# Two weights' low parts by accumulating DMA, and the decay table's sums one and a half products earlier, in a one-core Mamba-2 and band-attention step

## The chip, the cores and the metric

The program runs on 1 core of one Trainium2 chip. The metric is the time of one execution in microseconds (us), taken on the device; several executions are timed and their median is given. One more execution is profiled: its trace holds every instruction with start and duration, and all trace numbers below are from that one. Engines: PE is TensorE (matmuls; PEld its weight loads), DVE is VectorE, ACT is ScalarE, POOL is GpSimd, SP is the queue from which most DMAs are issued. Each engine works its own instructions in the order in which they were given to it.

## What is computed

A two-layer hybrid encoder advances one step: 1024 frames of a new stream and 64 frames of a running one, 1088 columns together, all in f32. Layer 0 is a Mamba-2 SSD mixer and a SwiGLU FFN, layer 1 is chunk-band attention and a SwiGLU FFN, with a shared K/V in between. The change lies at the head of layer 0:

```python
zxbcdt = u @ w_in                       # u = rmsnorm(x): z, x, B, C and dt are slices of it
conv = conv_b
for k in range(CONV_W):
    conv = conv + padded[:, k:k + L] * conv_w[k]
xbc = jax.nn.silu(conv)
...
dt = jax.nn.softplus(dt_raw + dt_bias)
dA = dt * A
Acs = jnp.cumsum(dA, axis=-1)           # within a chunk
Lm = jnp.exp(jnp.where(causal, Acs[..., :, None] - Acs[..., None, :], -jnp.inf))
y_diag = jnp.einsum('bcgjqs,bcsgjp->bcqgjp', CB[:, :, :, None] * Lm, xd)
decay_to_end = exp(Acs[..., -1:] - Acs)
chunk_states = einsum(Bc, xd * decay_to_end)
y_off = einsum(Cc, h_prev) * exp(Acs)
```

The tables of `dt`, of the sums `Acs` and of the decays are needed before any head's SSD work can begin.

## The kernel before, in words

**Products.** TensorE takes operands in a short format (float32r). So each f32 operand is split in a high part (rounded by ScalarE) and a low part (what is left over), and a product is three matmuls for each of the 8 blocks of the inner dimension: high weight by high u (L454), high weight by low u (L455), low weight by high u (L456), in this order. A *unit* is one 128-row weight tile by one slice of columns, 24 matmuls. There are three slices s = 0, 1, 2 with 384, 384 and 320 columns. A unit's result stands in one PSUM bank; the tag `mm` has two such banks, taken in turn, and the next unit that takes a bank must wait until the evacuation has read it. `scaled` (L721) evacuates: it multiplies the bank by the norm's row and writes SBUF. In slice 2 it takes two instructions for x, B and C, one for the new stream's 256 columns and one for the running stream's 64.

**Weights.** The class `Weights` streams weight tiles: SP loads a tile of 128x1024 f32 (512 KB) into one of two `raw` buffers (L252), ScalarE casts it to the high part (L340), VectorE subtracts to the low part (L341), both into one of three `hl` buffers; the `raw` buffer is free once both have read it. An `hl` buffer is free once the last unit that uses the weight is done. A weight planned with `acc` takes another way, in `part`: ScalarE casts (L334) and then writes minus the high part into the low part's place (L335), and GpSimd issues a DMA (L336) that reads the tile from HBM once more and adds it there. In the kernel before only the first weights of the FFNs are planned so, 12 tiles in all.

**Order of the weights.** First B0, C0 and x0 (in `w_in` the tiles 32, 36 and 16), all of which run slice by slice with the dt product between them. Then the groups of `order`: group 0 is x1 and z0, group 1 is x2 and z1, and so on. For group 0 the units come as x1 s0, x1 s1, z0 s0, z0 s1, z0 s2, x1 s2. x1's buffer is the one that B0 leaves, z0's the one that C0 leaves, x2's the one that x0 leaves.

**Order on TensorE.** TensorE's order is written out by hand: `Stream` keeps a planned time `st.t`, each unit adds its columns' cost to it, and at the half and the end of every unit side tasks whose due time has come put their instructions in between. A task yields its cost and the delay until its next step. The orders of the other engines are laid by a planner over the whole program, from its own costs, with priorities (`tc.high_priority`); it fills idle places with later instructions.

**The decay table.** `table_task` is such a side task. Its first step stands in the middle of B0's unit of slice 2: matmuls that turn the dt rows into columns (L678), and then, on VectorE at high priority, softplus (a polynomial of nine steps, L688, and L689 to L691, which write `t0`, the product of dt and A). It yields 1.0 with the delay `TB_V`. Its second step takes the sums, a matmul with a triangle of ones (`acsp`, L694), and VectorE copies them (`nac`, L696); 1.0 later the third takes the totals (`lastp`, L699) and nine transposes (`acT`, L707), whose rows ScalarE copies (L709) and SP stores to HBM (`ascr`, L710). 2.5 after that `tabs` lets the SSD tasks go.

**The SSD tasks.** `ssd_task(j, s)`, for head pair j and slice s, counted by q = 3j + s, first loads the sums' rows spread over the partitions (`MT`, L845, and `ea`, L848), makes decays of them (VectorE L854, ScalarE L855), and 8.0 later transposes x (`xtp`, L866), scales it (`xd`, VectorE L876; `xe`, GpSimd L877), masks the decays (`MT` by `CB`, L878), multiplies to the chunk states (`sp`, L885), and for two tasks at a time gives out the results (`yp` L816, `yo` L826). x1 s2's unit may not stand in TensorE's order before the results of q = 0 and q = 1. B and C are transposed and multiplied by `group_task` (`bnp` L785, `cbp` L791).

Of the kernel before, what the change touches and what calls it, by code (L numbers as in the profile page):

```python
# [44 lines left out]
AT_W1, AT_W2 = 6.0, 2.5  # L45
SSD_GAP, SSD_D = 4.4, 8.0
ST_W, ST_RB = (6.5, 22.0, 22.0), (6.0, 1.0, 1.0)
TB_W, TB_V = 1.0, 14.0
ES = 0.5, 0.5, 0.0
OS = 1.9, 1.4  # L50
EP_W, ER_W, EQ_W = (9.4, 9.4, 2.2), (8.9, 8.9, 3.3), (11.0, 11.0)
# [323 lines left out]
def hybrid_kernel(  # L375
# [28 lines left out]
    for _ in range(17):  # L404
# [14 lines left out]
    W = Weights(  # L419
        nc, Ring(wp, "raw", RAWB, [P, 1024]), Ring(wp, "hl", HLB, [P, 2, 1024], F32R),  # L420
        Ring(None, "half", 0, [P, 2, 512], F32R), Ring(None, "tt", 0, [P, 1024]),
    )
# [134 lines left out]
    order = []  # L557
# [8 lines left out]
            else:  # L566
                order.append((("x", 15), ("z", 14), ("z", 15)))
    W.plan(*[dict(src=[w_in[t]]) for t in (32, 36, 16)])
    for grp in order:
        W.plan(*[dict(src=[w_in[{"B": 32, "C": 36, "x": 16, "z": 0}[kd_] + i]]) for kd_, i in grp])  # L570

    MGS = ((0, 1, 2), (3, 4, 5), (6, 7))
    for b in range(2):
# [64 lines left out]
    with ExitStack() as es:  # L638
# [440 lines left out]
        for grp in order:  # L1079
# [9 lines left out]
            for i, s in seq:  # L1089
                kd_, jj_ = grp[i]  # L1090
# [5 lines left out]
                elif kd_ == "C" and q >= 5:  # L1096
                    g_, s_ = divmod(q - 5, 3)
# [904 lines left out]
```

## Time and profile before

| | |
|---|---|
| median of 3 runs | 2980.72 us (2979.49 to 2980.98) |
| the profiled execution | 2979.66 us, of which the trace's span is 2978.0 us |
| granted TensorE clock, mean over the span | 0.996 |
| busy share of the span | PE 98%, DVE 69%, ACT 47%, POOL 24% |
| instructions in the span | 56302 |

A busy PE is not a PE at its peak: matmuls that run at a lower granted clock count as busy too. Shares over the whole span say little about the stretch around the change, from 50 to 110 us, which is why the next part reads windows. In a list of instructions in order of time a row gives start, duration, engine, line, operation, what is written and read, how many were merged (x6), and in brackets the idle time of the engine before it and what ended that. In a list of waits a row gives who waited for whom, the total in us, the number of times and the longest. In a table of windows a row gives the stretch, its length, then for each engine its busy time and number of instructions, then TensorE's granted clock, the busy share of the DMA engines, and GB/s.

### The profile page before, as it was taken

The numbers are of one execution on the slowest core, as the hardware profiler recorded it, in microseconds if no ns is written. First come the engines' busy times: TensorE is split into PE (matmuls) and PEld (weight loads), VectorE is DVE, ScalarE is ACT, GpSimd is POOL, SyncE is SP. The second block draws the span as 40 slices with busy tenths as digits, with TensorE's granted clock in tenths as the row PEclk, the third lists the DMA queues.
The fourth block names the chain that finished last, engine by engine and source line by source line (L and its number), as shares of the span: only waits on it lengthen the run. The fifth ranks groups of instructions, "written<-read, shape, count | busy, mean of one in ns | idle before, by whom it ended". The sixth has DMA issues, their size and how long they took to land.

```text
span 2978.0 us, 56302 instructions
## 1 busy us (share of the span) xinstructions
PE 2921.0 (98%) x21626; PEld 2871.4 (96%) x21626; DVE 2040.2 (69%) x4471; ACT 1394.1 (47%) x2530; POOL 719.2 (24%) x821
## 2 busy tenths in 40 slices
PE   8999999999999999999999999999999999999999
PEld 7899999999999999999999899999999999999999
DVE  7887878885768545584567777777678645475544
ACT  6554646454453223344445665555653323244443
POOL 1333333331122343451111000000131343351111
PEclk9999999999999999999999999999999999999999
DMA  3333333244563222345665222223365222255654
GB/s 122 113 105 99 102 100 106 90 120 148 171 185 113 82 81 73 96 153 171 202 192 157 83 80 73 65 64 95 115 180 174 80 81 75 78 153 174 215 178 137
DMA packets 201551, 363.36 MB, mean 122 GB/s; under 512 B 20545, under 2 KB 149281, under 8 KB 201281
## 3 DMA queue, kind: packets, MB, share of 16 engines
q1 hardware_dynamic: 199488, 353.39, 38.6%
q0 software_dynamic: 1792, 6.36, 1.1%
q8 instruction: 170, 2.79, 0.4%
q14 instruction: 101, 0.82, 0.1%
HBM read 292.47 MB, written 62.74 MB: 119 GB/s over the span
## 4 chain that ended last, share of the span: by engine, by line
PE 83%; DVE 9%; DMA 3%; ACT 2%; issue 2%; POOL 0%; SPq 0%; DVEq 0%; ACTq 0%; POOLq 0%
PE px L1280 9%; PE px L1281 9%; PE px L1282 9%; PE mm L454 7%; PE mm L456 7%; PE mm L455 7%; PE po L1480 6%; PE po L1481 6%; PE po L1479 6%; PE mmx L455 3%; PE mmx L454 3%; PE mmx L456 3%; PE po L1763 2%; PE ptp L1724 1%; DVE sc L1702 1%
## 5 line engine op out<-in xcount | busy, mean ns | idle before, releaser
L454 PE MATMUL mm<-r,hl 128*128 128x384 f32 (+2 forms) x1664 | 555.2, 334 | 5.7 <-ACT BT L768 3.0
L456 PE MATMUL mm<-r,hl 128*128 128x384 f32 (+2 forms) x1664 | 539.0, 324 | 3.6 <-DVE hl L353 2.9
L455 PE MATMUL mm<-r,hl 128*128 128x384 f32 (+2 forms) x1664 | 537.8, 323 | 0.0
L341 DVE TENSOR_TENSOR hl<-raw,hl 128x1024 fp32r<-128x1024 f32 (+1 forms) x219 | 257.6, 1177 | 227.5 <-ACT hl L340 223.2
L1281 PE MATMUL px<-r,hl 128*128 128x288 f32 (+1 forms) x1184 | 347.3, 293 | 0.0
L454 PEld LDWEIGHTS mm<-r,hl 128*128 128x128 f32 x1664 | 314.7, 189 | 8.8 <-ACT BT L768 3.2
L456 PEld LDWEIGHTS mm<-r,hl 128*128 128x128 f32 x1664 | 313.9, 189 | 5.1 <-DVE hl L353 3.9
L455 PEld LDWEIGHTS mm<-r,hl 128*128 128x128 f32 x1664 | 315.0, 189 | 0.1
L1280 PE MATMUL px<-r,hl 128*128 128x288 f32 x1056 | 310.9, 294 | 0.0
L1282 PE MATMUL px<-r,hl 128*128 128x288 f32 x1056 | 310.7, 294 | 0.0
L340 ACT CAST hl<-raw 128x1024 fp32r<-128x1024 f32 (+1 forms) x219 | 219.9, 1005 | 176.1 <-PE po L1481 99.7
L480 POOL TENSOR_TENSOR ssum<-ssum,sq 128x256 f32<-128x256 f32 (+3 forms) x97 | 129.2, 1333 | 639.6 <-ACT sq L479 624.3
L1281 PEld LDWEIGHTS px<-r,hl 128*128 128x128 f32 x1184 | 222.3, 188 | 0.0
L1282 PE MATMUL px<-rx,hl 128*128 128x256 f32 x768 | 214.9, 280 | 6.6 <-DVE hl L341 6.6
L1280 PE MATMUL px<-rx,hl 128*128 128x256 f32 x768 | 215.4, 280 | 0.8 <-ACT hl L340 0.8
L1480 PE MATMUL po<-rx,hl 128*128 128x384 f32 (+1 forms) x624 | 201.5, 323 | 0.2 <-DVE rx L1344 0.2
L1280 PEld LDWEIGHTS px<-r,hl 128*128 128x128 f32 x1056 | 198.4, 188 | 0.2 <-DVE u L1295 0.2
L1282 PEld LDWEIGHTS px<-r,hl 128*128 128x128 f32 x1056 | 198.3, 188 | 0.0
L1479 PE MATMUL po<-rx,hl 128*128 128x384 f32 (+1 forms) x608 | 197.3, 324 | 0.0
L1481 PE MATMUL po<-rx,hl 128*128 128x384 f32 (+1 forms) x608 | 196.5, 323 | 0.0
L1281 PE MATMUL px<-rx,hl 128*128 128x256 f32 x640 | 178.7, 279 | 0.0
L290 POOL TENSOR_TENSOR tt<-raw 128x512 f32<-128x512 f32 x40 | 55.4, 1386 | 438.3 <-DMA raw<-in_w_f_dram 333.9
(359 smaller groups left out, 8052.6 us busy)
## 6 DMA issues: line engine op xcount, KB each, us to landing
raw<-in_w_f_dram SPq DMA_DIRECT2D x154, 512.0 KB, 3.8
rx<-in_w_f_dram SPq DMA_DIRECT2D x54, 512.0 KB, 3.7
raw<-in_w_in_dram SPq DMA_DIRECT2D x40, 512.0 KB, 3.6
MT<-ascr SPq DMA_DIRECT2D x48, 384.0 KB, 4.3
sg<-hscr SPq DMA_DIRECT2D x88, 192.0 KB, 3.5
raw<-in_w_f_dram SPq DMA_DIRECT2D x44, 384.0 KB, 3.4
raw<-in_w_so_dram SPq DMA_DIRECT2D x32, 512.0 KB, 4.0
raw<-in_w_kv_dram SPq DMA_DIRECT2D x18, 512.0 KB, 3.5
```

What stands on the lines that cost most here:

```text
L340: self.nc.scalar.copy(h, v)
L341: (eng or self.eng or self.nc.vector).tensor_tensor(lo, v, h, op=ALU.subtract)
L454: PE.matmul(ps[:, :n], h_, xh, start=(first and i == 0), stop=False)
L455: PE.matmul(ps[:, :n], h_, xl, start=False, stop=False)
L456: PE.matmul(ps[:, :n], l_, xh, start=False, stop=(last and i == nk - 1))
L480: (eng or G).tensor_tensor(ssum[:, :n], ssum[:, :n], q[:, :n], op=ALU.add)
L1280: PE.matmul(ps, wh, ah[:, k, :], start=(k == 0), stop=False)
L1281: PE.matmul(ps, wh, al[:, k, :], start=False, stop=False)
L1282: PE.matmul(ps, wl, ah[:, k, :], start=False, stop=(k == 3))
L1479: PE.matmul(ps[:, :n], wh, xh, start=(k == 0), stop=False)
L1480: PE.matmul(ps[:, :n], wh, xl, start=False, stop=False)
L1481: PE.matmul(ps[:, :n], wl, xh, start=False, stop=(k == FT - 1))
```

## The change

Two edits. The x1 and z0 weights (group 0 of `order`) are planned with `acc`: their low parts come by the way of L335 and L336 in place of L341. And the delay `TB_V` between the table's first and second step goes from 14.0 to 10.0 of the planned time, which changes the place of the sums, and of all that follows from them, in TensorE's order.

```diff
-TB_W, TB_V = 1.0, 14.0
+TB_W, TB_V = 1.0, 10.0
...
     W.plan(*[dict(src=[w_in[t]]) for t in (32, 36, 16)])
-    for grp in order:
-        W.plan(*[dict(src=[w_in[{"B": 32, "C": 36, "x": 16, "z": 0}[kd_] + i]]) for kd_, i in grp])
+    for g_, grp in enumerate(order):
+        W.plan(*[dict(src=[w_in[{"B": 32, "C": 36, "x": 16, "z": 0}[kd_] + i]], acc=g_ < 1) for kd_, i in grp])
```

The way that `acc` takes in `part` is in the kernel before already:

```python
        if it.get("acc"):
            with self.tc.high_priority(self.pri):
                self.nc.scalar.copy(h, v)
                self.nc.scalar.activation(lo, h, AF.Copy, scale=-1.0)
            self.nc.gpsimd.dma_start(lo, it["src"][0], accum_op=ALU.add)
            it[key] = h, lo
            return
```

## The prediction

> **What bounds the kernel now.** I read the page's chain first, then TensorE's waits in the stretch that the change touches (30 to 115 us), then windows of 3.41 us around these waits for the granted clock, then each engine's instructions in order of time.
>
> ```profile
> PE 83%; DVE 9%; DMA 3%; ACT 2%; issue 2%; POOL 0%; SPq 0%; DVEq 0%; ACTq 0%; POOLq 0%
> ```
>
> The chain that ends last is TensorE's for 83%. VectorE's work costs time only where TensorE waits for it, and time that TensorE saves early shortens the whole. Its waits between 30 and 115 us:
>
> ```profile
> PE sp L885 <- POOL xe L877: 3.7, 1, 3.7
> PE mm L454 <- ACT BT L768: 3.0, 1, 3.0
> ...
> PE sp L885 <- DVE xd L876: 1.8, 1, 1.8
> ```
>
> Two places, then: 3.0 us at the start of x1 s0, and 3.7 + 1.8 = 5.5 us at the first chunk states. Each is followed by a stretch at a lower clock (busy time, PEclk, DMA share, GB/s):
>
> ```profile
> 65.69:69.10 3.41, 0.57 (x4) 1.00 0.45 154
> 69.10:72.51 3.41, 3.26 (x13) 0.65 0.54 159
> 72.51:75.92 3.41, 3.41 (x21) 0.85 0.00 0
> 99.79:103.20 3.41, 1.59 (x12) 0.66 0.00 0
> 103.20:106.61 3.41, 3.41 (x29) 0.50 0.01 2
> 106.61:110.02 3.41, 3.41 (x27) 0.84 0.93 210
> ```
>
> Busy time by the missing clock is what the low clock cost: 3.26 x 0.35 + 3.41 x 0.15 = 1.65 us behind the first wait, 1.59 x 0.34 + 3.41 x 0.50 + 3.41 x 0.16 = 2.8 us behind the second. So 13.0 us are at stake in all: 4.65 at the first place, 8.3 at the second.
>
> **The first wait.** The engines in order of time:
>
> ```profile
> 66.21 0.41 DVE L721 TENSOR_TENSOR craw<-mm,rb 128x256 f32<-128x256 f32 x1
> ...
> 67.38 1.23 DVE L341 TENSOR_TENSOR hl<-raw,hl 128x1024 fp32r<-128x1024 f32 x1 [0.39 <-ACT hl L340]
> ...
> 68.89 0.22 DVE L721 TENSOR_TENSOR craw<-mm,rb 128x64 f32<-128x64 f32 x1
> ...
> 69.25 0.41 PE L454 MATMUL mm<-r,hl 128*128 128x384 f32 x1 [2.99 <-ACT BT L768]
> ...
> 69.67 0.34 PE L456 MATMUL mm<-r,hl 128*128 128x384 f32 x1
> ```
>
> The list names ScalarE's BT, but x1 s0 neither reads nor writes BT. It takes the bank that C0 had, and that bank's last reader is the 64-column evacuation, 68.89 + 0.22 = 69.11. The evacuation is late because VectorE does x2's low part (67.38) before it, and that had to wait for x0's end; its other half was late (66.21) because of x1's and z0's low parts and the table's polynomial.
>
> **The second wait:**
>
> ```profile
> 78.16 0.65 PE L694 MATMUL acsp<-tt,U 128*128 128x288 f32 x2
> 82.75 1.27 SPq L710 DMA_DIRECT2D ascr<-row  x3
> 84.79 0.38 SPq L845 DMA_DIRECT2D MT<-ascr  x1
> 94.48 1.27 DVE L854 TENSOR_SCALAR MT<-MT,nac 128x128 f32<-128x128 f32 x6 [0.27 <-DMA MT<-ascr]
> 95.06 0.82 PE L866 MATMUL xtp<-ident,xsT 128*128 128x128 f32 x6
> 97.97 1.01 DVE L876 TENSOR_TENSOR xd<-xtp,dt 128x384 f32<-128x384 f32 x2
> 98.67 2.34 POOL L877 TENSOR_TENSOR xe<-xd,dec 128x384 f32<-128x384 f32 x2 [16.59 <-DVE xd L876]
> 99.56 0.94 PE L885 MATMUL sp<-xe,Bn 128*128 128x128 f32 x6 [3.68 <-POOL xe L877]
> 102.63 1.62 PE L885 MATMUL sp<-xe,Bn 128*128 128x128 f32 x6 [1.82 <-DVE xd L876]
> ```
>
> xd waits on VectorE behind the decays (L854), which wait for MT's loads, which follow from the sums at 78.16.
>
> **Edit 1, the low parts.** Removed: two L341 on VectorE. Added: two negations on ScalarE, two DMA issues on GpSimd, two more reads of 512 KB.
>
> ```profile
> 58.62 1.05 ACT L340 CAST hl<-raw 128x1024 fp32r<-128x1024 f32 x1 [1.41 <-PE mmp L456]
> 59.57 0.65 ACT L759 ACTIVATE BT<-craw,pcs 128x323 f32<-128x323 f32 x1
> 60.29 1.22 DVE L341 TENSOR_TENSOR hl<-raw,hl 128x1024 fp32r<-128x1024 f32 x1
> 63.86 1.23 DVE L341 TENSOR_TENSOR hl<-raw,hl 128x1024 fp32r<-128x1024 f32 x1 [0.31 <-ACT hl L340]
> 66.69 0.35 POOL L755 COPY cst<-craw 128x3 f32<-128x3 f32 x1 [7.12 <-DVE craw L721]
> 70.56 0.45 DVE L691 TENSOR_TENSOR tt<-dt,negA 128x288 f32<-128x288 f32 x1
> ACT hl L340 <- PE mm L456: 5.0, 2, 2.6
> ```
>
> VectorE gains 1.22 + 1.23 + 0.31 of waiting = 2.8 us ahead of C0's evacuation. Brought forward by 2.8, the 64 columns would end at 66.3, when TensorE gets there; and x2's low part, which waits for x0's end, then stands behind them. So this wait goes, at the latest part of it. If the planner still puts x2 first, nothing is gained here: bounds 0 and 3.0. The two negations (1.04 each) fall into ScalarE's 5.0 us of waiting between the casts, GpSimd is idle for 7.12 us: both cost nothing there, and if that cover were gone ScalarE would be 2.1 later with slice 2's BT and CT, which TensorE takes up only at x1 s1. The `raw` buffer is free after the cast already, so x2's and z1's loads start 1 to 2 us earlier; nobody waits for these.
>
> What is late next is x1's own low part, which the third matmul of x1 s0 (69.67 now) needs. From the FFN's tiles:
>
> ```profile
> L335 ACT ACTIVATE hl<-hl x7: 1042/1043/1060, 853.8 to 2239.1; 128x1024 fp32r<-128x1024 f32 x7
> L336 POOL DMA_DIRECT2D hl<-in_w_f_dram x7: 849/867/876, 855.1 to 2240.5; - x7
> DMA to landing us min/median/max: 5.8/8.9/11.1
> raw<-in_w_in_dram SPq DMA_DIRECT2D x10, 512.0 KB, 3.9
> 61.50:67.30 5.80, 4.76 (x33) 4.50 (x31) 5.18 (x12) 2.05 (x2) 0.35 (x1) 1.00 0.46 135
> 2209.23:2215.03 5.80, 5.73 (x44) 5.76 (x45) 5.20 (x22) 4.73 (x9) 2.77 (x5) 1.00 0.92 228
> ```
>
> Cast to 59.67, BT (L759) slipped in between to 60.2, negation to 61.2, issue at 61.5. The landing is bounded by 3.9 (a plain load of the same tile) and 11.1. I take 5.8, the FFN's fastest, since it is the nearest: the other DMAs beside it took a share of 0.92, here they take 0.46. So the low part is there at 67.3 (65.4 to 72.6), and the third matmul starts 69.67 - 67.3 = 2.4 us earlier (3.0 earlier, when no wait is left, to 2.9 later). I book 2.3, and the 1.65 of clock, since 0.6 us of idle is left in place of 3.0. z0's low part (cast 4 us later) is needed two units later: nothing.
>
> The Trainium skill, "DMA: Bandwidth & Descriptors", section "Anatomy of one DMA", gives a DMA from GpSimd as 2.0 us plus the bytes over 436 GB/s, for 512 KB an estimate of 3.2 us. By that nothing is left of the wait and the sum below is 0.7 larger; the trace's own 5.8 to 11.1 for such a transfer disagree, and I go by them.
>
> **Edit 2, the sums.** In planned time, counted from the table's first step: its cost 1.0, B0's second half 1.63, C0 3.25, x0 3.25, x1 s0's first half 1.95 make 11.09. Due at 1.0 + 10 = 11.0, the sums now stand in the middle of x1 s0, ahead of `bnp`. Due at 15.0 they missed that place and x1 s0's end (14.02 with bnp and cbp), and came in the middle of x1 s1 (15.97). The totals and transposes go from x1 s1's end to x1 s0's end, `tabs` to the middle of x1 s1, with it the four MT and eight ea loads on SP, and the first `xtp` from z0 s2's end to the middle of z0 s1. The second xtp and the sp stay. No instruction is added.
>
> ```profile
> 72.47 0.84 PE L785 MATMUL bnp<-ident,BT 128*128 128x128 f32 x3
> ```
>
> So acsp moves from 78.16 to 72.47, 5.7 us ahead. Its input t0 was ready at 70.56 + 0.45 = 71.0, and 2.8 us earlier without the low parts, while the middle of x1 s0 comes at about 69: no wait. SP's queue holds nothing that would stop the stores and loads there, GpSimd's neither. The last decays, 94.48 + 1.27 now (one more task's follows), are done some 5 us sooner, ahead of xtp's 95.06. The first sp then finds its xe ready (its xtp stands 1.5 units ahead). The second needs xtp, xd (0.5), xe (2.34 / 2 = 1.2), about 1.9 with the handing over, beside 0.94 + 0.41 us of the first sp and the third xtp on TensorE: 0.6 left; I take 1.0, for VectorE is crowded there. 5.5 - 1.0 = 4.5 us. With 1.0 us idle I expect the clock to hold: 2.8 more. Bounds: 0 (VectorE holds xd as before) and 8.3.
>
> The Trainium skill, "TensorE: Matmul & The Clock Gate", section "Why this matters for your kernels", allows idle gaps of up to about 3 us before the clock falls. By that rule the first stretch's 1.65 us wouldn't be the 2.99 us gap's and would stay: a sum smaller by 1.65. The rows speak against it, 1.00 before that gap and 0.65 behind it.
>
> **The sum.** 2.3 + 1.65 + 4.5 + 2.8 = 11.25. From this comes what VectorE gives back once TensorE runs ahead: it is nearly full behind this stretch, and TensorE's waits there are of this size.
>
> ```profile
> 110.00:150.00 40.00, 40.00 (x296) 39.25 (x295) 37.79 (x98) 23.38 (x34) 18.91 (x27) 1.00 0.43 131
> PE xtp L866 <- DVE nv L498: 2.4, 3, 0.8
> ```
>
> I take 1.5 (0 to 2.4). 9.7 us remain. The profiled execution took 2979.66, 1.66 of it outside the span; 2969.9 follows, and as the median of the runs is 1.06 above the profiled one, 2971.0.
>
> **The rivals.**
> *x1's low part comes late.* At 11.1 us, or with the issue put behind the copy at 66.69 in GpSimd's order, the third matmul starts at 72.6: 2.9 lost, no clock back, the second place's 7.3 less 1.5 stays: 2.9 gained, 2978. Against it: the FFN's slow ones ran beside a full DMA. 17%.
> *VectorE holds the first states.* 5 us earlier sums do nothing if xd still stands behind decays in VectorE's order and a wait of 3.5 us with its low clock stays. Then the second place gives 5.5 - 3.5 = 2 of its 8.3, the first 3.95, less 1.5: 4.5 gained, 2976. For it: 37.79 of 40 us. 15%.
> *Slower: the planner lays the SSD loop anew.* VectorE's, ScalarE's and GpSimd's orders come from one plan, which starts from other times now. If in the loop of 48 SSD tasks TensorE meets one more short wait at each, such as the xtp waits on the norm's steps (three in 290 us now, up to 0.8), 0.2 us a task eat the 9.7; at 0.5 us the loss is 24 - 9.7 = 14 and the time 2995. Against it: TensorE's order in the loop keeps its places, since all due times shift together. 10%.
>
> **How the numbers follow.** The forecast has 58%, its own range 2967.8 (13.0 gained, nothing given back) to 2974. The range, 2966 to 2979.5, takes in the first two rivals and 2 us of a luckier plan. 0.2% is 6 us, about what a measurement can tell. Faster by that: nearly all of the forecast, a fifth of the two small-gain rivals, 61%; within it 33%; slower 6%.
>
> **What would show it.** Right: the 64-column evacuation ahead of x2's low part on VectorE; TensorE's wait at x1 s0 under 1.5 us, on the accumulating DMA; acsp in the middle of x1 s0; MT loads near 77 us; waits before sp of 1 us in all; the clock 1.00 from 66 to 110. Wrong: that DMA landing after 69.7, xd still behind the decays, or new waits in the loop after 110 us.

## The result, and the profile after

The changed kernel takes 2971.76 us, the median of 7 runs (2970.04 to 2976.18); the kernel before, run beside it, takes 2981.54 us, the median of 7 (2979.49 to 2983.44). The ratio is 0.9969, with an interval of 0.9959 to 0.9979: 9.2 us less, between 6 and 12. The profiled execution took 2972.53 us. The prediction was 2971.0 us (2966.0 to 2979.5).

The page of the kernel after, busy time, share and instructions of each engine:

```profile
PE 2920.7 (98%) x21626; PEld 2871.0 (97%) x21626; DVE 2033.7 (68%) x4469; ACT 1395.0 (47%) x2532; POOL 715.7 (24%) x823
```

Nothing in these shares tells of 9 us. TensorE's waits between 30 and 115 us do (a row of 2.4 us at `nbp` and one of 1.0 at `craw`, both ahead of the stretch that the change touches, are left out):

```profile
PE xtp L866 <- ACT zs L948: 1.0, 1, 1.0
...
PE sp L885 <- DVE hn L898: 0.6, 1, 0.6
PE cbp L791 <- DVE Bn L786: 0.4, 1, 0.4
PE mm L456 <- DMA hl<-in_w_in_dram: 0.3, 1, 0.3
```

Of 8.5 us of waiting at the two places, 1.9 are left: 0.34 at x1 s0 and 1.57 before the chunk states. A new wait of 0.35 stands at `cbp`.

**The first place.** The engines of the kernel after, in order of time (this profiled execution came to the table's first matmul, L678, 0.65 us later than the one of before: 54.20 against 53.55, so its times compare with those shown of before after taking off 0.65):

```profile
59.30 1.05 ACT L334 CAST hl<-raw 128x1024 fp32r<-128x1024 f32 x1 [1.44 <-PE mmp L456]
60.25 0.66 ACT L759 ACTIVATE BT<-craw,pcs 128x323 f32<-128x323 f32 x1
60.81 1.04 ACT L335 ACTIVATE hl<-hl 128x1024 fp32r<-128x1024 f32 x1
...
62.16 0.90 POOL L336 DMA_DIRECT2D hl<-in_w_in_dram  x1 [1.92 <-ACT hl L335]
...
64.67 0.22 DVE L721 TENSOR_TENSOR craw<-mm,rb 128x64 f32<-128x64 f32 x1
...
66.76 0.34 PE L454 MATMUL mm<-r,hl 128*128 128x384 f32 x1
67.61 0.44 PE L456 MATMUL mm<-r,hl 128*128 128x384 f32 x1 [0.34 <-DMA hl<-in_w_in_dram]
68.14 0.46 DVE L691 TENSOR_TENSOR tt<-dt,negA 128x288 f32<-128x288 f32 x1
68.52 1.22 DVE L341 TENSOR_TENSOR hl<-raw,hl 128x1024 fp32r<-128x1024 f32 x1
69.46 0.65 PE L694 MATMUL acsp<-tt,U 128*128 128x288 f32 x2
```

C0's last evacuation ends at 64.9, almost 2 us before TensorE begins x1 s0 at 66.76, and x2's low part (68.52) now stands behind it and behind `t0` (L691) as well. What TensorE waits for is x1's own low part, 0.34 us. `acsp` finds `t0` ready: 68.14 + 0.46 = 68.6, needed at 69.46. How long the two accumulating DMAs took from issue to landing (line L336 of the kernel after, between 55 and 75 us; the shorter one is x1's, issued at 62.16):

```profile
DMA to landing us min/median/max: 5.4/6.0/6.5
```

**The second place**, in order of time:

```profile
75.95 0.38 SPq L845 DMA_DIRECT2D MT<-ascr  x1
...
87.25 1.26 DVE L854 TENSOR_SCALAR MT<-MT,nac 128x128 f32<-128x128 f32 x6 [0.49 <-DMA MT<-ascr]
...
91.07 2.55 DVE L878 TENSOR_TENSOR MT<-MT,CB 128x640 f32<-128x640 f32 x3
92.80 0.83 PE L885 MATMUL sp<-xe,Bn 128*128 128x128 f32 x6
93.54 0.48 DVE L721 TENSOR_TENSOR zs<-mm,rb 128x320 f32<-128x320 f32 x1
93.94 0.54 DVE L876 TENSOR_TENSOR xd<-xtp,dt 128x384 f32<-128x384 f32 x1
94.63 0.52 PE L866 MATMUL xtp<-ident,xsT 128*128 128x128 f32 x3 [1.00 <-ACT zs L948]
95.72 0.91 PE L885 MATMUL sp<-xe,Bn 128*128 128x128 f32 x6 [0.57 <-DVE hn L898]
```

The fourth task's decays (87.25) are done at 88.5; before, the third task's were done at 95.75 and the fourth's began only at 96.80. The first `sp` (92.80) waits for nothing. The second `xd` (93.94) stands behind the masks (L878) and z0's evacuation, and the third `xtp` needs the bank that this `xd` reads: 93.94 + 0.54 = 94.48, and it starts at 94.63. The list names ScalarE's `zs`, which does not read that bank; in a second execution of this kernel (e11) it names `xd` for the same wait.

The granted clock around both places, in windows of 3.41 us (busy time, PEclk, DMA share, GB/s):

```profile
66.55:69.96 3.41, 3.07 (x18) 1.00 0.98 251
...
93.83:97.24 3.41, 2.04 (x21) 1.00 0.00 0
97.24:100.65 3.41, 3.41 (x38) 1.00 0.49 130
```

The clock stays at 1.00 where it had been 0.50 to 0.85.

**What VectorE gives back.** The prediction booked 1.5 us for it. Read between 110 and 400 us, TensorE's waits come to 3.8 us where they had been 2.6, which looks like 1.2 given back. But the window's edge makes that difference. Before and after, TensorE waits six times for 0.80 us at `xtp` until the end of the mixer; since the kernel after is ahead, one of the six comes in front of 400 us that stood behind it, the kernel before first:

```profile
405.14 0.52 PE L866 MATMUL xtp<-ident,xsT 128*128 128x128 f32 x3 [0.80 <-DVE nv L498]
```

and the kernel after:

```profile
396.14 0.52 PE L866 MATMUL xtp<-ident,xsT 128*128 128x128 f32 x3 [0.80 <-DVE nv L498]
```

Only the short waits at `mm` differ (0.17 + 0.33 us before, 0.28 + 0.33 after): 0.1 us is given back.

So the terms come out as 2.65 (2.99 - 0.34) and 1.65 of clock at the first place, 3.9 (5.5 - 1.57) and 2.8 of clock at the second, together 11.0, less 0.35 at `cbp` and 0.1 given back: 10.55. The 2.8 is read from windows that lie across the edges of the low clock; half of TensorE's busy time between these edges (100.86 to 107.68 us, 1.64 + 3.41) makes 2.5, and the sum 10.3.

### The profile page after: what moved, and what is told of

It is laid out like the page before. It is cut to its first block, busy times and chain, and to the rows that moved or that the text cites. A ratio compares the mean times of both kernels' runs of the same rounds, so it can differ in the third digit from the quotient of the medians.

```text
span 2970.8 us, 56314 instructions
## 1 busy us (share of the span) xinstructions
PE 2920.7 (98%) x21626; PEld 2871.0 (97%) x21626; DVE 2033.7 (68%) x4469; ACT 1395.0 (47%) x2532; POOL 715.7 (24%) x823
## 4 chain that ended last, share of the span: by engine, by line
PE 82%; DVE 10%; DMA 3%; ACT 2%; issue 2%; SPq 0%; POOL 0%; DVEq 0%; ACTq 0%; POOLq 0%
PE px L1280 9%; PE px L1281 9%; PE px L1282 9%; PE mm L454 7%; PE mm L456 7%; PE mm L455 6%; PE po L1480 6%; PE po L1481 6%; PE po L1479 6%; PE mmx L455 3%; PE mmx L454 3%; PE mmx L456 3%; PE po L1763 1%; PE ptp L1724 1%; DVE sc L1702 1%
## 5 line engine op out<-in xcount | busy, mean ns | idle before, releaser
L454 PE MATMUL mm<-r,hl 128*128 128x384 f32 (+2 forms) x1664 | 554.7, 333 | 3.1 <-DVE craw L721 1.3
L341 DVE TENSOR_TENSOR hl<-raw,hl 128x1024 fp32r<-128x1024 f32 (+1 forms) x217 | 254.1, 1171 | 226.9 <-ACT hl L340 225.8
L454 PEld LDWEIGHTS mm<-r,hl 128*128 128x128 f32 x1664 | 314.9, 189 | 5.6 <-DVE craw L721 1.3
```

Of the source, the lines that this page charges most:

```text
L341: (eng or self.eng or self.nc.vector).tensor_tensor(lo, v, h, op=ALU.subtract)
L454: PE.matmul(ps[:, :n], h_, xh, start=(first and i == 0), stop=False)
```

## The experiments

Theory: the two edits remove two separate stalls, the first one a PSUM bank whose reader stands behind low parts on VectorE, the second one decays that come late, each with the low clock behind it, and their gains add. Its rivals were asked one at a time. Beside the median stands a second measure, which leaves out what differs from execution to execution before the change and far behind it: the stretch from the table's first matmul (L678) to the first matmul of the FFN's tile `mmx` (L454), in the profiled execution. The medians of before that belong to the three groups of runs are 2980.90 (e1 to e4), 2980.11 (e5 to e8) and 2980.55 (e9 to e12).

| kernel | median us | ratio [interval] | L678 start | first mmx | stretch | against 659.3 |
|---|---|---|---|---|---|---|
| before | 2981.54 | 1 | 53.55 | 712.89 | 659.3 | |
| after | 2971.76 | 0.9969 [0.9959, 0.9979] | 54.20 | 703.33 | 649.1 | -10.2 |
| e1 low parts alone | 2976.36 | 0.9982 [0.9973, 0.9991] | 52.81 | 708.35 | 655.5 | -3.8 |
| e2 sums alone | 2975.37 | 0.9981 [0.9972, 0.9989] | 54.23 | 707.02 | 652.8 | -6.5 |
| e3 C0's evacuation first | 2976.14 | 0.9982 [0.9973, 0.9990] | 52.55 | 707.65 | 655.1 | -4.2 |
| e4 low parts on GpSimd | 2977.32 | 0.9983 [0.9975, 0.9992] | 54.11 | 708.84 | 654.7 | -4.6 |
| e5 e3 and the sums | 2975.84 | 0.9982 [0.9973, 0.9991] | 55.62 | 707.54 | 651.9 | -7.4 |
| e6 sums earlier still | 2970.85 | 0.9968 [0.9957, 0.9979] | 55.12 | 704.31 | 649.2 | -10.1 |
| e7 stores beside x1's DMA | 2977.91 | 0.9992 [0.9983, 1.0001] | 54.04 | 710.41 | 656.4 | -3.0 |
| e8 xd first | 2970.36 | 0.9966 [0.9953, 0.9978] | 53.14 | 702.10 | 649.0 | -10.4 |
| e9 x1 alone | 2972.36 | 0.9971 [0.9959, 0.9983] | 53.75 | 702.23 | 648.5 | -10.9 |
| e10 z0 alone | 2972.28 | 0.9972 [0.9961, 0.9984] | 52.99 | 703.96 | 651.0 | -8.4 |
| e11 after, once more | 2971.86 | one run | 55.54 | 704.66 | 649.1 | -10.2 |
| e12 before, once more | 2978.32 | one run | 55.07 | 711.66 | 656.6 | -2.7 |

The last row says how far the stretch can be trusted: two executions of the kernel before differ by 2.7 us in it. The rows of e9 and e12 are 1.7 us too good, since a low clock behind the table's first matmuls, which most executions have, is missing there (see e11 and e12). It is missing in e10 too, where a longer low clock near 660 us takes 1.3 of it back; in e1 and e5 that longer one makes the rows 1.0 and 0.9 too bad.

### One edit alone (e1, e2)

e1 is the kernel after without the second edit:

```diff
-TB_W, TB_V = 1.0, 10.0
+TB_W, TB_V = 1.0, 14.0
```

> Edit 1 alone: x1's and z0's low parts by accumulating DMA, the sums where they were before (TB_V 14). Theory (two places that add up): the wait at the start of x1 s0 falls from 3.0 to about 0.3 us and the 1.65 us of low clock behind it go; the waits before sp stay at about 5.5 us with their low clock, since the decay table's chain keeps its place relative to TensorE's order. About 4 us faster than before, ratio 0.9986. Rival (the edits hang together: TensorE that comes sooner only waits longer before sp): the waits before sp grow to 8 us or more, ratio 0.9995 to 1.000.

e2 is the kernel before with the second edit alone:

```diff
-TB_W, TB_V = 1.0, 14.0
+TB_W, TB_V = 1.0, 10.0
```

> Edit 2 alone: TB_V 10, all low parts by VectorE. Theory: the wait of 3.0 us at the start of x1 s0 stays; the sums' input t0 is ready at about 71.0 us and the sums stand at about 72.5, so TensorE does not wait for it; the waits before sp fall from 5.5 to 1 to 2 us and the clock stays at 1.00 there. About 6.5 us faster than before, ratio 0.9978. Rival (VectorE, still with the two low parts, has the table late or holds xd as before): a new wait before acsp or 3 us and more before sp, ratio 0.999 or above.

TensorE's instructions with a wait, e1 (start, duration, and the wait in brackets):

```profile
66.29 0.44 PE L456 MATMUL mm<-r,hl 128*128 128x384 f32 x1 [0.42 <-DMA hl<-in_w_in_dram]
94.45 1.65 PE L885 MATMUL sp<-xe,Bn 128*128 128x128 f32 x6 [3.44 <-POOL xe L877]
```

The same of e2:

```profile
69.93 0.41 PE L454 MATMUL mm<-r,hl 128*128 128x384 f32 x1 [2.99 <-ACT BT L768]
98.01 0.55 PE L866 MATMUL xtp<-ident,xsT 128*128 128x128 f32 x3 [0.78 <-DVE xd L876]
```

And the clock in the window behind the wait that each of them keeps, e1's first:

```profile
93.83:97.24 3.41, 2.29 (x9) 0.50 0.01 2
```

e2's:

```profile
69.96:73.37 3.41, 3.41 (x13) 0.59 0.45 159
```

Each edit removes its own wait with its own low clock and leaves the other. By the ratios 5.4 + 5.7 = 11.1 us (intervals of 2.7 to 8.0 and 3.3 to 8.3) against 9.2 for both; by the stretch 3.8 + 6.5 = 10.3 against 10.2. So the gains add, as far as intervals of 5 us and a stretch that is good to 2.7 can tell; the waits show it more sharply. In e1 the waits left before `sp` are 3.44 and 0.79 us, 4.2 in all and not the 5.5 expected. In e2 the low clock of the second place is gone with the long waits, though 0.78 us remains at `xtp` and 0.63 at the `sp` behind it.

### Is it the bank, and not what the list names? (e3)

The list puts the 2.99 us down to ScalarE's `BT`. e3 is the kernel before, with all low parts on VectorE, and only a higher priority for C0's last evacuation:

```diff
-                    scaled(raw[:, 3:259], ps_, s, 0, 256)
-                    scaled(raw[:, 262:326], ps_, s, 256, 64)
+                    with tc.high_priority(HIP if ct == 20 else 0):
+                        scaled(raw[:, 3:259], ps_, s, 0, 256)
+                        scaled(raw[:, 262:326], ps_, s, 256, 64)
```

> The kernel before with one thing changed: C0's evacuation in slice 2 (two L721) gets the high priority, so that VectorE does it ahead of z0's and x2's low parts; no accumulating DMA, the sums stay. Theory (the first wait is for the bank that C0's evacuation frees, and that stands behind low parts): TensorE's wait at the start of x1 s0 goes altogether, 3.0 to about 0, and so do 1.65 us of low clock, about 4.6 us faster, ratio 0.9985, the waits before sp stay. Rival (the list of waits names the right one, ScalarE's BT, or VectorE's work as such is the limit and something else is late next): 2 us and more are left of the wait, ratio 0.9995 or above.

VectorE's and TensorE's instructions in order of time, e3 (lines behind the edit are one higher):

```profile
62.57 0.22 DVE L721 TENSOR_TENSOR craw<-mm,rb 128x64 f32<-128x64 f32 x1
...
71.00 0.41 PE L454 MATMUL mm<-r,hl 128*128 128x384 f32 x1 [0.54 <-DVE craw L721]
```

No wait at x1 s0; 0.54 us at x1 s1, which takes x0's bank. VectorE's order alone cured the first place; no instruction was added, taken away or moved to another engine, so the cause is the bank. The waits before `sp` stay (4.52 and 1.47 us). The gain, 0.9982 and 4.2 us of the stretch, is that of e1.

### What the accumulating DMA is good for (e4, e5)

If priority does as much as a DMA, is the DMA needed? e5 puts the second edit beside e3's priority, without any accumulating DMA for x1 and z0:

```diff
-TB_W, TB_V = 1.0, 14.0
+TB_W, TB_V = 1.0, 10.0
...
+                    with tc.high_priority(HIP if ct == 20 else 0):
```

> C0's evacuation first (as in the run with that alone) and TB_V 10, all low parts by VectorE. Theory (edit 1 also buys VectorE's time for the table; edit 2 alone had the cover of the 3.0 us wait at x1 s0): without that wait TensorE comes to the sums 14.8 us behind the table's first matmuls, while t0 was ready only 17.7 us behind them in the run with C0 first; so a wait of about 3 us appears before acsp in place of the one at x1 s0, and its low clock stays. The waits before sp fall to 1 to 2 us. In all like edit 2 alone, ratio 0.998. Rival (the two gains simply add): no wait at acsp over 0.5 us, ratio 0.9962 to 0.9968.

The row of e5 that decides:

```profile
73.39 0.75 PE L694 MATMUL acsp<-tt,U 128*128 128x288 f32 x2 [2.95 <-DVE tt L691]
```

Here the gains do not add: 2975.84, no better than e3 or e2 alone, and 7.4 us of the stretch (8.3 without its longer low clock near 660 us) where e3 and e2 make 10.7. With three low parts still on VectorE `t0` is ready only at 72.88 + 0.45, and `acsp`, moved forward, waits for it. The low clock that was expected behind this wait did not come in the profiled execution (the last part says why). So the first edit also pays for the second: it takes off VectorE the work that stood before `t0`.

e4 takes the low parts of x1 and z0 from VectorE in another way, by subtracting on GpSimd:

```diff
-            (eng or self.eng or self.nc.vector).tensor_tensor(lo, v, h, op=ALU.subtract)
+            (eng or self.eng or (self.nc.gpsimd if it.get("gl") else self.nc.vector)).tensor_tensor(lo, v, h, op=ALU.subtract)
...
-        W.plan(*[dict(src=[...], acc=g_ < 1) for kd_, i in grp])
+        W.plan(*[dict(src=[...], gl=g_ < 1) for kd_, i in grp])
```

> The changed kernel, but x1's and z0's low parts are subtracted by GpSimd from the loaded tile, in place of negation and accumulating DMA. Theory (what counts is that VectorE is rid of them, not the DMA): x1's low part is ready about 3 us after the cast, at 63 us, before TensorE needs it; no wait at x1 s0; the rest as in the changed kernel; the same within 2 us, ratio to before 0.9965 to 0.9972. Rival (GpSimd's subtraction is slow or slows VectorE beside it): VectorE's or GpSimd's work runs late and waits of 2 us and more come back at x1 s0 or before acsp, ratio 0.998 or above.

e4's instructions in order of time:

```profile
60.49 3.56 DVE L688 SCALAR_TENSOR_TENSOR dec<-dec,tt 128x288 f32<-128x288 f32 x3
60.83 2.42 POOL L341 TENSOR_TENSOR hl<-raw,hl 128x1024 fp32r<-128x1024 f32 x1 [0.20 <-ACT hl L340]
...
64.49 2.67 POOL L341 TENSOR_TENSOR hl<-raw,hl 128x1024 fp32r<-128x1024 f32 x1 [1.24 <-ACT hl L340]
64.80 2.70 DVE L761 SCALAR_TENSOR_TENSOR BT<-craw,pcs,BT 128x323 f32<-128x323 f32 x1
...
69.33 0.21 DVE L721 TENSOR_TENSOR craw<-mm,rb 128x64 f32<-128x64 f32 x1
69.69 0.41 PE L454 MATMUL mm<-r,hl 128*128 128x384 f32 x1 [2.84 <-DVE craw L721]
```

The same instructions in the kernel after, where GpSimd only issues:

```profile
60.11 1.45 DVE L688 SCALAR_TENSOR_TENSOR dec<-dec,tt 128x288 f32<-128x288 f32 x3
61.47 0.55 DVE L761 SCALAR_TENSOR_TENSOR BT<-craw,pcs,BT 128x323 f32<-128x323 f32 x1
```

Beside each subtraction on GpSimd the row of VectorE is 2.1 us longer (3.56 against 1.45, 2.70 against 0.55). Together that is 4.3 us, more than the 2.4 us that VectorE was spared; the bank is free at 69.5, counted from the table's first matmul within 0.2 us of before the change, and the wait of 2.84 us is back, this time under its right name. The rival was right here: relief by GpSimd is no relief. The Trainium skill, "SBUF — State Buffer", section "Who interferes with whom", says that a VectorE instruction with two SBUF inputs and a GpSimd instruction that reads SBUF shut each other out for a whole instruction; the trace agrees, L688 and L761 both being of that kind.

### One tile of the two (e9, e10)

The kernel after, with the accumulating DMA for x1's tile alone (e9) or z0's alone (e10):

```diff
-        W.plan(*[dict(src=[...], acc=g_ < 1) for kd_, i in grp])
+        W.plan(*[dict(src=[...], acc=g_ < 1 and kd_ == "x") for kd_, i in grp])
```

> The changed kernel with x1's low part alone by accumulating DMA, z0's by VectorE again. Theory (VectorE's relief ahead of the sums is what counts, both tiles alike): the sums' input t0 comes 1.2 to 1.5 us later than in the changed kernel, about 15.8 us behind the table's first matmuls, TensorE is at the sums at 15.3: a wait of about 0.7 us before acsp; C0's evacuation is still in time; about 0.7 us slower than the changed kernel, 9.5 us gained from the table's first matmul to the first mmx, ratio to before 0.9969. Rival (z0's share is what brought C0's evacuation forward): a wait of 1.5 us and more at the start of x1 s0 and the low clock again, 7 us gained or less.

> The changed kernel with z0's low part alone by accumulating DMA, x1's by VectorE again. Theory: as with x1 alone, t0 about 1.2 us later, about 15.5 us behind the table's first matmuls, but no landing to wait for at the third matmul of x1 s0 (0.3 us): TensorE comes to the sums at about 15.0, a wait of 0.5 to 0.8 us; 9.5 us gained from the table's first matmul to the first mmx, ratio to before 0.9969. Rival: as for x1 alone.

TensorE's wait before the sums, e10:

```profile
67.93 0.75 PE L694 MATMUL acsp<-tt,U 128*128 128x288 f32 x2 [1.67 <-DVE tt L691]
```

Both ratios (0.9971, 0.9972) lie within the interval of the kernel after. Either tile's relief, 1.2 us, is enough for the bank: x1 s0 waits 0.24 us for it in e9 and not at all in e10. At `acsp` e9 waits 0.24 us. In e10 x1's low part still stands ahead of `t0`, which costs 1.67 us at `acsp`; I had expected half of that. The low parts of z0 in e10 landed only 8.1 us after their issue and nobody waited for them. These runs can't tell the second accumulating DMA from nothing.

### The landing (e7)

The prediction's largest rival was a late landing. e7 is the kernel after with four stores of 512 KB on SP beside x1's accumulating DMA; they compute nothing and only keep the DMA engines busy:

```diff
+            for d_ in it.get("beside", ()):
+                self.nc.sync.dma_start(d_, h.bitcast(F32))
```

> The changed kernel with four stores of 512 KB each (x1's high part to HBM memory that layer 1 overwrites later) issued on SP right after x1's cast, beside the accumulating DMA; they compute nothing. Theory (what is late next is x1's low part, and its landing grows with the traffic beside it): the DMA lands 9 us or more after its issue, not 5.4; TensorE waits 3 us or more at the third matmul of x1 s0 and the clock falls behind it; everything behind is later by 4 us or more than in the changed kernel, ratio 0.998 to 0.999. Rival (an accumulating DMA takes its 5 to 6 us whatever runs beside it): landing under 7 us, wait under 1.5 us, ratio 0.997.

From issue to landing in e7 (the lines are two higher here):

```profile
DMA to landing us min/median/max: 8.0/9.4/10.8
```

And its TensorE:

```profile
70.12 0.44 PE L458 MATMUL mm<-r,hl 128*128 128x384 f32 x1 [3.01 <-DMA hl<-in_w_in_dram]
```

x1's low part, issued at 62.0, lands 8.0 us later in place of 5.4, and TensorE waits 3.01 us at the matmul where the kernel after waits 0.34; windows with a clock of 0.59 and 0.91 follow. At the second place `xtp` waits 1.86 us in place of 1.0, with windows of 0.59 and 0.91 behind it again. Why `xtp` waits longer is not shown. Nearly all of the gain is lost (0.9992, 0.9983 to 1.0001). So there is no margin at this place: the landing came 2.6 us later, and TensorE waits 2.7 us more.

### The sums earlier still, and xd first (e6, e8)

e6 is the kernel after with the sums due another 2.0 sooner:

```diff
-TB_W, TB_V = 1.0, 10.0
+TB_W, TB_V = 1.0, 8.0
```

> The changed kernel with TB_V 8 in place of 10: the sums one place earlier, at x0's end, ahead of x1 s0. Theory (the sums may move only as far as t0 is ready): t0 is ready 14.4 us behind the table's first matmuls, TensorE is there after 12.7: a wait of about 1.8 us before acsp, x1's low part has then landed; before sp little is left to gain, since that wait is for the second xd, whose xtp keeps its place. 1 to 2 us slower than the changed kernel, ratio to before 0.9973. Rival (earlier is better still): ratio 0.9960 to 0.9966.

e6's TensorE:

```profile
69.65 0.72 PE L694 MATMUL acsp<-tt,U 128*128 128x288 f32 x2 [1.82 <-DVE tt L691]
96.70 0.91 PE L885 MATMUL sp<-xe,Bn 128*128 128x128 f32 x6 [0.74 <-DVE xd L876]
```

The 1.8 us at `acsp` came as expected; the slower time did not. x1's low part and `cbp` are no longer waited for, since TensorE is held up ahead of both, and of the 1.57 before `sp` only 0.74 remain: 2.56 us of waiting in all where the kernel after has 2.26. A wait put in one place took two others away.

e8 is the kernel after with `xd` of q = 1 at high priority:

```diff
-            V.tensor_tensor(hd(xd), hd(pt[:, :384].rearrange("p (a b) -> p a b", b=P)), tb(dt), op=ALU.mult)
+            with tc.high_priority(HIP if q == 1 else 0):
+                V.tensor_tensor(hd(xd), hd(pt[:, :384].rearrange("p (a b) -> p a b", b=P)), tb(dt), op=ALU.mult)
```

> The changed kernel with the second xd (L876 of q = 1) at high priority on VectorE, ahead of the masks and z's evacuation. Theory (the 1.0 and 0.6 us of waiting before the third xtp and the second sp are for VectorE's xd, whatever the list of waits names): the wait at xtp goes, in all 0.6 us or less is left, 1 us faster than the changed kernel, ratio to before 0.9963 to 0.9968. Rival (the wait named, for ScalarE's zs): the waits stay at 1.5 us.

Its VectorE and TensorE:

```profile
90.35 2.55 DVE L879 TENSOR_TENSOR MT<-MT,CB 128x640 f32<-128x640 f32 x3
92.83 0.54 DVE L877 TENSOR_TENSOR xd<-xtp,dt 128x384 f32<-128x384 f32 x1
93.52 0.52 PE L866 MATMUL xtp<-ident,xsT 128*128 128x128 f32 x3 [0.52 <-DVE xd L877]
```

`xd` went ahead of the evacuation but not of the masks, whose three instructions were laid before its `xtp` was there. The wait at `xtp` is half as long (0.52 against 1.00), under the right name now, which confirms whose bank it is; the one at the second `sp` is 0.74 (0.57 in the kernel after), and the one at x1's low part is 0.78 in this execution. The two waits before the second `sp` thus keep 1.26 us where 0.6 or less was expected. 2970.36 can't be told from the kernel after.

### Both kernels once more (e11, e12)

> The changed kernel once more, for what differs between two executions of one program. If the 2 us that its first profile lost against before inside the attention stage are a matter of the execution, they are not lost here, and the gain of 10 us between the table's first matmul and the first mmx comes again within 0.5 us. If they come from the change, they are lost again.

> The kernel before once more, for the same purpose: the waits of 3.0, 3.7 and 1.8 us come again within 0.5 us, the start of the table's matmuls may differ by 1 us (52.6 to 55.6 in the runs so far).

The lead of after over before in the first pair of profiles is 712.89 - 703.33 = 9.6 us at the first `mmx` and 2978.0 - 2970.8 = 7.2 at the end. In this pair it is 711.66 - 704.66 = 7.0 and 2976.6 - 2970.2 = 6.4. So the 2.4 us that the first pair loses behind the Mamba mixer belong to those executions and not to the change: in the first profile of after the clock is low for 3.41 us from 1671.59 and again from 2292.82, which costs 1.7 us each, and neither e11 nor the two profiles of before have these two. The gain of 10 us did not come again within 0.5 us, though that was expected: by the stretch this pair makes 7.5, and the difference lies in before. Its waits before `sp` were 4.29 and 0.79 us here, where 3.7 and 1.8 within 0.5 were expected. Why the stretch of before is shorter shows in the clock behind the table's first matmuls, e12:

```profile
58.51:61.92 3.41, 3.41 (x25) 1.00 0.00 0
```

and at the same place in e11:

```profile
58.88:62.29 3.41, 3.41 (x15) 0.50 0.00 0
```

There the clock falls in most executions of either kernel, for 3.41 x 0.50 = 1.7 us, and in three (e9, e10, e12) it doesn't. That is 1.7 of the 2.7 us; the waits before `sp`, 5.1 in place of 5.5, and a wait of 0.33 at 516 us that e12 doesn't have make up most of the rest.

## Why the prediction was right, point by point

| step of the prediction | predicted | measured |
|---|---|---|
| the wait at x1 s0 is C0's bank, not `BT` | gone when VectorE is relieved | gone; e3 removes it by order alone |
| negations and issues cost nothing | 0 | no wait on either; `BT` stands between cast and negation as said |
| x1's low part lands | 5.8 us after the issue, with a DMA share of 0.46 beside it | 5.4, with a share of 0.87 (e7: 8.0 with stores beside, at a full share) |
| first wait | 2.3 gained, 0.6 left | 2.65 gained, 0.34 left |
| clock behind it | 1.65 | 1.65 |
| `acsp` | about 69, no wait | 69.46 (68.8 on the clock of before), no wait |
| `MT` loads | near 77 | 75.95 |
| waits before `sp` | 4.5 gained, 1.0 left | 3.9 gained, 1.57 left |
| clock behind them | 2.8 | none is left; 2.8 by the prediction's windows, 2.5 between the edges |
| given back behind 110 us | 1.5 | 0.1, and 0.35 at `cbp` |
| sum | 9.7 | 10.3 by the terms; 10.2 by the stretch; 9.2 (6 to 12) by the ratio |

The mechanism was right at both places. Two terms were not, and they cancel in part, which is luck.

**The term that was too good** is the second place: 0.6 us worked out, 1.0 taken, 1.57 measured. The step counted only `xtp`, `xd` and `xe` and put the crowding of VectorE at 0.4. The rows show what stands there: three masks of 0.85 us and z0's evacuation ahead of the second `xd`, then a wait for the bank of `sp`, which VectorE's `hn` (L895, L898) reads, 0.57 us that the long waits of before had hidden.

**The term that was too dear** is the 1.5 us given back: 0.1 was, and 0.35 at `cbp`. The 2.4 us of waits that it was read from are a fixed part of the mixer, the same six waits of 0.80 in either kernel, and do not grow when TensorE runs ahead. The first place came out 0.35 better too, because the landing was at 5.4.

**What was right for a fuller reason than the prediction gave.** It said that the moved sums find `t0` ready because the low parts are gone, and booked nothing for it. e5 shows that this is a term of its own: without the DMAs `acsp` waits 2.95 us. The terms add for these two edits because one edit covers the other's cost; with priority in place of the DMA they don't.

**The rivals.** A late landing did not come about, though the DMA engines were busy for 0.87 of the time beside it and not for the 0.46 that the prediction had read from the kernel before. e7 made one: 2977.91 us, where 2978 was worked out for a landing 11.1 us after the issue, 3.1 later than e7's; part of e7's loss lies at the second place, which that working had left alone. VectorE does hold `xd`, for 1 us and not for 3.5. New waits in the SSD loop did not appear: 0.1 us between 110 us and its end.

**What is not settled.** The terms make 10.3, the stretch 10.2 and the medians 9.2; the 1.0 between is below what two executions of one kernel differ by.

## What to carry to other kernels

When TensorE waits at the start of a product, ask which bank it takes and who reads that bank last, and look on that engine for what stands ahead of the reader; the name in the list of waits may be only what ended at the same moment. Before work is moved from a crowded engine, try whether an order alone removes the wait (e3: as much as the DMA), then look for the second customer of the relief (`t0`: there the order alone failed). And a stage's work that is moved forward is limited by its inputs' engine: each of the places tried for the sums that came before VectorE was through (e5, e6, e10) showed up as a wait at `acsp` of 1.7 to 3.0 us. Last, compare waits one by one and not by their sum between two fixed times: a change that brings everything forward moves waits across the edge of such a window.

## What the runs showed of the hardware

- In e4 a GpSimd subtraction of 128x1024 (2.42 and 2.67 us) held up VectorE's two-input instruction beside it by 2.1 us each time, which cost VectorE more than the 1.2 us of its own subtraction.
- An accumulating DMA of 512 KB landed 5.4 us after its issue at a DMA share of 0.87, and 8.0 with 2 MB of stores beside it, at a full share (1.02 in the profile). z0's took 6.5 us in the kernel after and 8.1 in e10.
- The granted clock fell to 0.50 behind waits of 2.84 (e4), 2.99 (before, e2, e12) and 3.01 us (e7), and not behind 1.82 (e6), nor behind 2.95 us in e5. What decides is where the wait lies. In each trace the clock changes only at edges that are whole multiples of 3.413 us apart (in before at 56.48, 70.14 and 100.86 us, 4 and 9 of them), and the low clock follows a period between two edges in which TensorE was idle for more than about half. Before (length, busy time, clock as above):

```profile
66.72:70.14 3.42, 0.89 (x5) 1.00 0.53 156
70.14:73.55 3.41, 3.41 (x14) 0.50 0.35 135
```

and e5, where an edge cuts the 2.95 us in two:

```profile
68.47:71.88 3.41, 1.97 (x12) 1.00 0.47 161
71.88:75.29 3.41, 1.90 (x11) 1.00 0.39 141
```

Idle for 2.53 us of a period, before lost the clock; idle for 1.44 and 1.51, e5 kept it. In all fourteen traces, the first 4 us and the case of the next point aside, every period at full clock with 1.89 us or more of idle time was followed by a low one, and none with less than 1.70; between the two both occur. So whether one wait costs the clock differs between executions of one program. The prediction weighed a rule of the Trainium skill, "TensorE: Matmul & The Clock Gate", section "Why this matters for your kernels", that allows gaps of about 3 us; here 2.84 was too long, and the 1.65 us came back as booked.
- A busy TensorE can lose its clock too. The 18 matmuls of 64x32 with which the table begins take 2.19 us, without a gap in the trace. In the eleven executions in which they lie whole in one such period, the clock was 0.50 in the next; in the three in which an edge cuts them (e9, e10, e12) it stayed at 1.00. In e12 the edge cuts off only the first 0.03 us, so this is a pattern in the traces, and its cause is not shown.
